# A Hymba layer on one Trainium2 core: the FFN of all four row groups by a seven-product scheme, with the products of plain weights placed beside the attention

## The chip, the core and the metric

The kernel runs on one core of a Trainium2 chip. A core has five engines that each work through their own queue in order: TensorE (PE in the profile; its weight loads are listed as PEld), VectorE (DVE), ScalarE (ACT), GpSimd (POOL) and SyncE (SP), which here issues all the transfers between DRAM and the on-chip memory. Sixteen DMA engines carry them out. The metric is device time in microseconds, lower is better. The kernel before takes 2677.42 us, the median of three runs (2672.66 to 2678.96).

## The reference

One decoder layer on 2048 rows of 1024 float32 values. Cut to what is computed:

```python
a = rmsnorm(x, g_pre_mix); u = a @ w_in                 # 1024 -> 2560
conv  = silu(layernorm(depthwise_conv31(u_val * sigmoid(u_gate)) + b))   # 512 channels
for each head and each query t:                          # 8 heads x 64
    z = q.k / 8
    A[t,s] = sigmoid(z_ts) * prod_{s<j<t} (1 - sigmoid(z_tj)),  s < t
    attn = A @ v, then a head-wise rmsnorm
h = x + rmsnorm(concat(conv, attn) @ w_out, g_post_mix)
f = rmsnorm(h, g_pre_ffn)
out = h + rmsnorm((silu(f @ w_gate) * (f @ w_up)) @ w_down, g_post_ffn)   # 1024 -> 2816 -> 1024
```

A head's attention needs a running product along each row of scores. VectorE does it with a scan, which stands between the two sigmoids on ScalarE and the multiplication on GpSimd.

## The kernel before, in words

**Precision.** Every float32 matrix product is done as three products of rounded halves (high and low part of both operands, without low by low). So a weight tile of 128 x 1024 is loaded, rounded on ScalarE and its rest taken on GpSimd (`load_w`, lines 193 to 210). The two halves are kept in DRAM and loaded from there at the next use. `Weights` (lines 212 to 225) loads two tiles ahead, into rings of three buffers.

**Row groups.** The 2048 rows are four groups of 512 rows. For each group: `prep` (operand columns), `inproj` as `gv` (gate and value of the convolution) and `qkv`, `taps` and `convnorm` (the convolution: 31 multiply-adds per channel block on VectorE, lines 437 to 485), `attn`, `mix`, `outproj`, `residual`, and the FFN.

**Attention** (lines 505 to 642). Group g has 8 heads with g+1 key blocks each; one block of 512 keys and 128 queries is called a block here, and there are 320 of them (32, 64, 96 and 128 for the four groups). A block takes: two score products (lines 533 and 536) into one of two banks `z`; two sigmoids on ScalarE (541, 543); a scan on VectorE (545); a multiplication on GpSimd (546); four transposes on TensorE (562); the rounding of the result on ScalarE and its rest on VectorE (229, 230); two products with the values (567, 568).

**The FFN of groups 0 and 1** is `ffn` (lines 701 to 844), as written: 72 products of 512 columns per 128 hidden channels (24 gate, 24 up, 24 down), 22 such steps, so 1584 for each group.

**The FFN of groups 2 and 3** is `ffn_pair` (lines 882 to 1195). The two groups are the two halves of one matrix product, which is split 2 x 2 and done by Strassen's scheme in Winograd's form: seven products instead of eight, on sums of the weights' quarters and of the inputs' quarters. The products are numbered 1 to 7 as in the code. Products 1 and 2 take plain quarters of weights and inputs; 4 takes the plain quarter 22 of the weights; 3, 5, 6 and 7 take sums of weights (lines 937 to 940). A step of gate or up is 84 products, and there are 22; the down product follows in 77 slots of 12 products (lines 1144 to 1195). Together 2772.

**The order of the work.** The table `PLAN` lists the pieces of the main chain (in-projections, out-projections, FFN). `beside` (lines 113 to 126) runs a piece step by step and lets two side chains go on: the attention of all groups and the taps. Two numbers in each row of PLAN say how far each side goes in that piece; the attention's scale (line 1204) makes its whole length 351 of these units, and the rows share them out from `prep` 0 to the last `ffn` 1. When attention and taps are over, `mix` 3 and `outproj` 3 run beside the rest of `ffn` 1 (lines 1266 to 1280), then come the pair's input sums and the pair. A scheduler orders each engine's queue afterwards from this program order; that order is fixed in the built program.

Of the kernel before, what the change touches and what calls it, by code (L numbers as in the profile page):

```python
# [19 lines left out]
P = 128  # L20
# [20 lines left out]
    ("prep", 0, 4.4, 81, ("scaled", 0, 0, 0)),  # L41
    ("gv", 0, 0, 9),
    ("qkv", 0, 0, 13, ("stats", 1, 2, 2), ("turned", 1, 15, 2)),
    ("qkv", 0, 0, 0),
    ("prep", 1, 2.4, 8),
    ("gv", 1, 10.1, 18, ("stats", 2, 0, 3)),
    ("qkv", 1, 9.9, 34),
    ("qkv", 1, 1.1, 41, ("turned", 2, 10, 6)),
    ("mix", 0, 0, 15),
    ("prep", 2, 0, 0),  # L50
    ("out", 0, 28.7, 39),
    ("qkv", 2, 7.3, 16),
    ("qkv", 2, 3.1, 19, ("residual", 0, 1, 3)),
    ("gv", 2, 25.6, 61, ("stats", 3, 0, 2)),
    ("mix", 1, 0, 1),
    ("out", 1, 0, 47, ("turned", 3, 4, 8)),
    ("prep", 3, 0, 20),
    ("qkv", 3, 5.4, 10, ("hscaled", 0, 7, 0)),
    ("qkv", 3, 0, 45),
    ("gv", 3, 14, 12, ("residual", 1, 1, 2)),  # L60
    ("fprep", 0, 12.8, 19),
    ("ffn", 0, 32.8, 16),
    ("ffn", 0, 38.2, 24),
    ("ffn", 0, 11.8, 10),
    ("ffn", 0, 20.7, 0),
    ("mix", 2, 0.6, 0),
    ("out", 2, 17.6, 0, ("hscaled", 1, 1, 0)),
    ("fprep", 1, 19.2, 0, ("residual", 2, 18, 5)),
    ("ffn", 1, 27.5, 55),
    ("ffn", 1, 26.8, 63),  # L70
    ("ffn", 1, 28.9, 45),
    ("ffn", 1, 103.6, 66),
)
LATE = 1.14
# [55 lines left out]
def layer_kernel(ctx: ExitStack, tc: tile.TileContext, x, xT, g_pre_mix, w_in, conv_w, conv_b, ln_g, ln_b,  # L130
# [129 lines left out]
    fup = C.enter_context(tc.tile_pool(name="hidden", bufs=2))  # L260
# [63 lines left out]
    def turned(T):  # L324

        g, kp = divmod(T, TT)
        if kp == 0:
            assert need(*[("stats", g * TT + t) for t in range(TT)])()
            ps = bank("tps")
            for t in range(TT):  # L330
                q = g * TT + t
                nc.tensor.transpose(ps[:, t * P:(t + 1) * P], rstd1[:, q:q + 1].to_broadcast([P, P]), id32)
            rb = fup.tile([P, G], F32, tag="uH", name="rb")
            nc.scalar.activation(rb, ps, AF.Copy)
            rbs[g] = rb
# [167 lines left out]
    pinned = [False]  # L503

    def attn(g):
# [20 lines left out]
        def scores(u, j):  # L526
# [6 lines left out]
            mz = nc.tensor.matmul(z[:, 0:w], hd_["QL"][:, js], K[:, 0:w], start=True, stop=False)  # L533
            if pinned[0]:
                tc.keep_in_program_order(mz)
# [165 lines left out]
    def ffn(g0, NT, fx, acc, up, banks, og_=lambda: ev("og"), junk_=lambda: ev("junk", BF16), more=None, rows_=None):  # L701

        two = more is not None
        pairs = not two
        HT = NT * TT
        aH = [lambda k, t=t: fx[t][0][k // 4][:, k % 4, :] for t in range(NT)]
        aL = [lambda k, t=t: fx[t][1][k // 4][:, k % 4, :] for t in range(NT)]  # L710
        srcs = []
        for f in range(NF):
            if pairs:
                srcs += [(w_gate, f), (w_up, f)] + ([(w_down, f - 1), (w_down, f)] if f % 2 else [])
            else:
                srcs += [(w_gate, f)] + ([(w_down, f - 1)] if 0 < f < NF - 1 else []) + [(w_up, f)]
        wts = Weights(srcs + ([] if pairs else [(w_down, NF - 2)]))

        def down(parts, f, tts):

            end = f + len(parts) == NF

            def block(ps, i, tt, e):
                uH, uL, WH, WL_ = parts[i]
                us = slice(tt * P, (tt + 1) * P)
                es = slice(e * G, (e + 1) * G)
                nc.tensor.matmul(ps, uL[:, us], WH[:, es], start=i == 0, stop=False)  # L727
                nc.tensor.matmul(ps, uH[:, us], WH[:, es], start=False, stop=False)  # L728
                nc.tensor.matmul(ps, uH[:, us], WL_[:, es], start=False, stop=i == len(parts) - 1)  # L729

            first = {}
            if len(parts) > 1:
                for tt, e in [(tt, e) for tt in tts for e in range(2)][:2]:
                    first[tt, e] = bank("dps")
                    block(first[tt, e], 0, tt, e)
            for tt in tts:
                ss = sp.tile([P, 2], F32, tag="ss2", name="ss2", bufs=4) if end else None
                og = []
                for e in range(2):
                    es = slice(e * G, (e + 1) * G)  # L740
                    begun = (tt, e) in first
                    ps = first[tt, e] if begun else bank("dps")
                    for i in range(begun, len(parts)):
                        block(ps, i, tt, e)
                    if f == 0:
                        nc.vector.tensor_copy(acc[tt][:, es], ps)
                    else:
                        nc.vector.tensor_tensor(acc[tt][:, es], ps, acc[tt][:, es], ALU.add)
                    if end:
                        og.append(tail(tt, e, ss))  # L750
                if end:
                    finish(tt, ss, og)
# [589 lines left out]
```

## Time and profile before

| | before |
|---|---|
| median of three runs | 2677.42 us (2672.66 to 2678.96) |
| profiled execution, its own time | 2676.57 us |
| span of that execution, first to last instruction | 2674.6 us |
| TensorE busy | 2508.3 us (94%) |
| VectorE, ScalarE, GpSimd busy | 1813.2, 1069.4, 1314.5 us (68%, 40%, 49%) |
| DMA | 556.79 MB, 208 GB/s |
| mean granted TensorE clock | 0.974 |

A row of instructions in the profile names line, engine, operation, output<-input and shape, then count, busy time and mean duration in ns, then the idle time before them and what ended it. A row of the windows names a stretch of the span, then for each engine the busy time and, in brackets, the count of instructions in it; after these stand the granted TensorE clock (1 is full speed), the busy share of the DMA engines and the rate in GB/s. Matmuls are pipelined, so the busy time of TensorE is not its work: how many it starts says more.

### The profile page before, as it was taken

To read this page: it belongs to the slowest core of one execution; us is meant where nothing else is said; L and a number is where in the kernel's file an instruction comes from. 1 tells how busy PE (TensorE), PEld (TensorE's weight loads), DVE (VectorE), ACT (ScalarE), POOL (GpSimd) and SP (SyncE) were. 2 spreads that over 40 slices of the span, in tenths; PEclk is the share of its full clock that TensorE was granted. 3 is DMA by queue.
4 is the path that set the end of the run, shared out by engine and by line. 5 is a ranking of instruction groups with operands and counts; after the bars stand their busy time and mean duration, and the time that the engine had idled before them with its cause. 6 is when DMAs were issued, how large, how long until landed. Compare 5 with 4: busy or idle time off the path is not lost.

```text
span 2674.6 us, 34465 instructions
## 1 busy us (share of the span) xinstructions
PE 2508.3 (94%) x11552; PEld 2031.6 (76%) x11552; DVE 1813.2 (68%) x2400; ACT 1069.4 (40%) x1979; POOL 1314.5 (49%) x1641
## 2 busy tenths in 40 slices
PE   8999999999999999999999999999657999999998
PEld 6788787778777787777778778887535888887886
DVE  6966698779866767554878898553257656665556
ACT  3444544454345555334564333331232222223543
POOL 4624533453155566545563322320267777674556
PEclk9999998999999999999999999999878999999999
DMA  8996776746776666666764444534433444447564
GB/s 323 347 321 229 237 265 203 258 147 225 245 281 220 229 245 232 233 244 249 252 234 170 162 169 153 186 135 177 162 117 107 135 168 161 158 142 263 189 185 170
DMA packets 200512, 556.79 MB, mean 208 GB/s; under 512 B 24720, under 2 KB 24720, under 8 KB 200336
## 3 DMA queue, kind: packets, MB, share of 16 engines
q1 hardware_dynamic: 200336, 554.61, 60.3%
q8 instruction: 91, 1.49, 0.2%
q14 instruction: 85, 0.70, 0.1%
HBM read 382.28 MB, written 172.23 MB: 207 GB/s over the span
## 4 chain that ended last, share of the span: by engine, by line
PE 63%; DVE 7%; POOL 4%; DMA 3%; ACT 2%; issue 2%; SPq 0%; POOLq 0%; DVEq 0%; ACTq 0%
PE p L950 15%; PE dps L950 7%; PE pg L237 3%; PE pg L241 3%; PE pg L239 3%; PE pu L237 3%; PE pu L239 3%; PE pu L241 3%; PE dps L727 2%; PE at L562 2%; PE dps L729 2%; PE dps L728 2%; DVE om L545 2%; PE inps L237 2%; PE inps L239 2%
## 5 line engine op out<-in xcount | busy, mean ns | idle before, releaser
L546 POOL TENSOR_TENSOR A<-A,om 128x512 f32<-128x512 f32 (+2 forms) x320 | 313.5, 980 | 663.0 <-DVE om L545 616.4
L545 DVE TENSOR_TENSOR_SCAN om<-om,one,z 128x513 f32<-128x513 f32 (+2 forms) x320 | 352.6, 1113 | 99.7 <-ACT A L543 97.7
L452 DVE SCALAR_TENSOR_TENSOR cv<-glu,cw,cv 128x512 f32<-128x512 f32 x464 | 347.2, 748 | 7.9
L206 POOL TENSOR_TENSOR wL<-raw,wH 128x1024 fp32r<-128x1024 f32 x94 | 224.6, 2394 | 143.2 <-ACT wH L205 138.3
L541 ACT ACTIVATE om<-z 128x512 f32<-128x512 f32 (+2 forms) x320 | 171.2, 536 | 249.1 <-PE z L536 149.4
L237 PE MATMUL inps<-xH,wL 128*128 128x512 f32 x640 | 258.9, 405 | 4.5 <-DVE vt L230 3.7
L239 PE MATMUL inps<-xH,wH 128*128 128x512 f32 x640 | 254.7, 399 | 0.0
L241 PE MATMUL inps<-xL,wH 128*128 128x512 f32 x640 | 254.2, 398 | 0.0
L230 DVE TENSOR_TENSOR TL<-at,TH 128x512 fp32r<-128x512 f32 (+1 forms) x320 | 187.7, 597 | 49.7 <-ACT TH L229 48.8
L229 ACT ACTIVATE TH<-at 128x512 fp32r<-128x512 f32 (+1 forms) x320 | 167.8, 545 | 122.3 <-PE at L562 117.6
L562 PE MATMUL at<-idr,A 128*128 128x128 f32 x1088 | 191.9, 276 | 4.8 <-DVE ot L584 2.4
L727 PE MATMUL dps<-wH,uL 128*128 128x512 f32 x352 | 150.0, 426 | 29.4 <-DVE uL L803 23.1
L543 ACT ACTIVATE A<-z 128x512 f32<-128x512 f32 (+2 forms) x320 | 169.7, 539 | 18.4 <-PE at L562 18.4
L562 PEld LDWEIGHTS at<-idr,A 128*128 128x128 f32 x1088 | 139.3, 142 | 41.2 <-POOL A L546 5.2
L1117 DVE TENSOR_TENSOR xLb<-lateL0b,xHb 128x512 fp32r<-128x512 f32 x77 | 99.1, 1294 | 90.9 <-ACT xHb L1116 90.9
L1115 POOL TENSOR_TENSOR t1b<-lateH0b,t0b 128x512 fp32r<-128x512 f32 x77 | 103.4, 1346 | 103.9 <-ACT t0b L1114 99.8
L205 ACT ACTIVATE wH<-raw 128x1024 fp32r<-128x1024 f32 x94 | 98.7, 1059 | 124.5 <-PE pu L241 32.6
L237 PEld LDWEIGHTS inps<-xH,wL 128*128 128x128 f32 x640 | 123.6, 193 | 30.1 <-issue 4.5
L237 PE MATMUL pu<-xH,wL 128*128 128x512 f32 x352 | 141.2, 401 | 3.9 <-DMA wL<-wL 3.2
L237 PE MATMUL pg<-xH,wL 128*128 128x512 f32 x352 | 140.9, 400 | 4.1 <-DMA wL<-wL 3.7
L241 PEld LDWEIGHTS inps<-xL,wH 128*128 128x128 f32 x640 | 123.1, 192 | 26.2
L239 PEld LDWEIGHTS inps<-xH,wH 128*128 128x128 f32 x640 | 123.5, 193 | 24.3
(308 smaller groups left out, 6559.3 us busy)
## 6 DMA issues: line engine op xcount, KB each, us to landing
wH<-wH SPq DMA_DIRECT2D x244, 512.0 KB, 4.5
wL<-wL SPq DMA_DIRECT2D x244, 512.0 KB, 4.1
raw<-in_w_gate_dram SPq DMA_DIRECT2D x44, 512.0 KB, 4.7
raw<-in_w_up_dram SPq DMA_DIRECT2D x44, 512.0 KB, 4.1
raw<-in_w_down_dram SPq DMA_DIRECT2D x44, 512.0 KB, 5.0
K<-kd SPq DMA_DIRECT2D x80, 256.0 KB, 4.1
V<-vd SPq DMA_DIRECT2D x80, 256.0 KB, 3.9
lateL0b<-ud SPq DMA_DIRECT2D x77, 256.0 KB, 2.7
```

The source lines that it names most:

```text
L206: nc.gpsimd.tensor_tensor(L, raw, H.bitcast(F32), ALU.subtract)
L230: nc.vector.tensor_tensor(L, ps, H.bitcast(F32), ALU.subtract)
L237: nc.tensor.matmul(ps, WL[:, kc], aH[t](k), start=k == 0, stop=False)
L239: nc.tensor.matmul(ps, WH[:, kc], aH[t](k), start=False, stop=False)
L241: nc.tensor.matmul(ps, WH[:, kc], aL[t](k), start=False, stop=k == KT - 1)
L452: nc.vector.scalar_tensor_tensor(to, gl[c][:, k:k + G], cw[:, c, k:k + 1], a, ALU.mult, ALU.add))
L541: nc.scalar.activation(om[:, G - w:G], z[:, 0:w], AF.Sigmoid, scale=-0.125)
L545: nc.vector.tensor_tensor_scan(r, r, z[:, 0:1].to_broadcast([P, w + 1]), one, ALU.mult, ALU.bypass)
L546: nc.gpsimd.tensor_tensor(a[:, 0:w], a[:, 0:w], om[:, G - w + 1:G + 1], ALU.mult)
L562: nc.tensor.transpose(pt[:, j * P:(j + 1) * P], u["A"][j][:, b * P:(b + 1) * P], id32)
L727: nc.tensor.matmul(ps, uL[:, us], WH[:, es], start=i == 0, stop=False)
L950: tc.keep_in_program_order(nc.tensor.matmul(ps, a, b, skip_group_check=True, **flags))
```

## The change

All four groups' FFN is done in two pairs (groups 0 and 1; groups 2 and 3) by the seven-product scheme. `ffn` and `ffn_pair` go. What is new:

- `c11(g)`: products 1 and 2 of gate and up for one pair, 528 products of 512 columns (11 steps of 48). Their results, product 1 alone and the sum of both, are copied by ScalarE into tiles of a ring of four (`ev`) and stored to DRAM, four tiles of 256 KB a step. `Weights(..., 1)` loads one tile ahead.
- `sums()`: the sums of weights, made once by GpSimd (132 operations on 128 x 512), stored, and loaded again by both pairs. It is a third side chain.
- `input_sums(g, k)`: the input sums of one pair, in four steps. Each step reads four stored pieces and stores twelve tiles, all sixteen through the ring `ev`.
- `five(g, B, todo)`: products 6, 5, 7, 3 and 4 of a step of gate or up, 60 products of 512 columns, 22 steps for a pair, with the stored sums rounded again and the results of `c11` loaded. The residuals of group 3 and the second pair's input sums run inside the first pair's steps.
- The down product of both pairs in one loop of 154 slots of 12 products.
- `PLAN` has one cost per piece instead of shares. A side chain's goal is now read off a line over the sum of these costs: ATTN runs straight from 0 at cost 80 to 1 at cost 832. The scales of the sides are given as reciprocals of their lengths; the attention's is the third line from the end of the diff below. With the yields of `attn` (unchanged), 32 x 128 for a whole unit of 512 keys and 20 x 128 for a diagonal one, the length is 2 x NH x P x sum(16 g + 10).

```diff
-    ("qkv", 3, 5.4, 10, ("hscaled", 0, 7, 0)),
-    ("qkv", 3, 0, 45),
+    ("qkv", 3, 66, ("residual", 1, 1, 3)),
+    ("fprep", 0, 6),
+    ("c11", 0, 120, ("residual", 2, 1, 1), ("hscaled", 1, 5, 0), ("tprep", 0, 6, 2), ("hscaled", 2, 19, 0)),
+    ("fprep", 2, 6),
+    ("c11", 2, 120),
...
+ATTN = ((80, 0.0), (832, 1.0))
+TAPS = ((50, 0.0), (205, 0.168), (230, 0.25), (385, 0.418), (394, 0.5), (545, 0.668), (558, 0.75), (832, 1.0))
+SUMS = ((130, 0.0), (820, 1.0))
...
+    def c11(g):
+        Hs, Ls = fx[g]
+        wts = Weights([(w, j) for j in range(HF) for w in W], 1)
+        for j in range(HF):
+            ws = [wts.next(), wts.next()]
+            pss = [bank("c11") for _ in W]
+            for hf in range(2):
+                for i, ps in enumerate(pss):
+                    WH, WL = ws[i]
+                    for k in range(4):
+                        kc = slice((4 * hf + k) * P, (4 * hf + k + 1) * P)
+                        matmul(ps, WL[:, kc], Hs[hf][:, k, :], start=hf == 0 and k == 0, stop=False)
+                        matmul(ps, WH[:, kc], Hs[hf][:, k, :], start=False, stop=False)
+                        matmul(ps, WH[:, kc], Ls[hf][:, k, :], start=False, stop=k == 3)
+                    c = ev("c")
+                    nc.scalar.activation(c, ps, AF.Copy)
+                    store(c, "c11", g, i, j, hf)
+                    yield 0.5
...
+    def input_sums(g, k, tmp):
...
+        def piece(k, i):
+            t = ev("piece")
+            nc.sync.dma_start(t, stored["fx", g, k, i])
+            return t
+        def halves(n, t):
+            H, L = ev("bH", F32R), ev("bL", F32R)
+            nc.scalar.activation(H, t, AF.Copy)
+            nc.vector.tensor_tensor(L, t, f32(H), sub)
+            store(f32(H), "B", g, n, k, 0)
+            store(f32(L), "B", g, n, k, 1)
...
+    attn_s = Side(chain(attn(g) for g in range(NG)), 1 / (8 * NH * P * sum(16 * g + 10 for g in range(NG))))
+    taps_s = Side(chain(taps(g) for g in range(NG)), 1 / (NG * (CB * CW + LAG * 3 * (1 + TT))))
+    sums_s = Side(sums(), 1 / (12 * HF))
```

What this does to the queues shows at two places. TensorE, in the attention of group 3. In the program before, score products `z`, value products `o` and transposes `at` stand among the FFN's down products `dps`:

```order
L568 MATMUL o<-TL,V 128x512
L533 MATMUL z<-K,QL 128x512
L536 MATMUL z<-K,QH 128x512
L533 MATMUL z<-K,QL 128x512
L536 MATMUL z<-K,QH 128x512
L562 MATMUL at<-idr,A 128x128 x5
L727 MATMUL dps<-wH,uL 128x512
L728 MATMUL dps<-wH,uH 128x512
L729 MATMUL dps<-wL,uH 128x512
L727 MATMUL dps<-wH,uL 128x512
L728 MATMUL dps<-wH,uH 128x512
L729 MATMUL dps<-wL,uH 128x512
```

The same engine at the same score product in the changed program:

```order
L534 MATMUL z<-K,QL 128x512
L535 MATMUL z<-K,QH 128x512
L566 MATMUL o<-TH,V 128x512
L534 MATMUL z<-K,QL 128x512
L535 MATMUL z<-K,QH 128x512
L567 MATMUL o<-TL,V 128x512
L561 MATMUL at<-idr,A 128x128 x4
L534 MATMUL z<-K,QL 128x512
L535 MATMUL z<-K,QH 128x512
L561 MATMUL at<-idr,A 128x128 x2
L534 MATMUL z<-K,QL 128x512
```

Nothing but attention stands here: its 320 blocks come ahead of out-projection 2 and of all of `c11`, and 202 of them stand in six runs with no other product between them (in the program before, 6 blocks stand so).

SyncE, beside the first pair's `c11` and `input_sums` in the changed program (`c` are the stored products, `B` the input sums, `fx` the pieces, `wH` and `wL` the kept halves of weights):

```order
L732 DMA c_0_1_2_1_14666<-c 128x512
L211 DMA wL_14747<-wL 128x1024
L211 DMA wH_14756<-wH 128x1024
L206 DMA raw<-in_w_up_dram 128x1024
L732 DMA B_3_0_0_14697<-bH 128x512
L211 DMA wL_14757<-wL 128x1024
L732 DMA B_3_0_1_14699<-bL 128x512
L206 DMA raw<-in_w_gate_dram 128x1024
L732 DMA B_5_0_0_14705<-bH 128x512
L732 DMA B_5_0_1_14707<-bL 128x512
```

and where the program before loads and stores the plain FFN's weights of group 0, among the attention's loads (`K`, `V`, `Q`):

```order
L209 DMA wH_9294<-wH 128x1024
L515 DMA QH<-qd_2_190 64x512 x2
L516 DMA QL<-qd_2_190 64x512
L209 DMA wL_9295<-wL 128x1024
L204 DMA raw<-in_w_gate_dram 128x1024
L523 DMA V<-vd_2_198 128x512
L522 DMA K<-kd_0_149 128x512
L209 DMA wH_9304<-wH 128x1024
```

The loads of weights stand now behind stores that wait for ScalarE and VectorE, and no attention work stands between them on any queue.

776 lines of the change are left out of this document (312 added, 464 removed).

## The prediction

> **What bounds the kernel now.** First the page's top line and its first part, then the windows cut where the attention's last scan ends (1771 us) and where TensorE comes to full speed again. Columns of a window: length, then busy time and count for PE, PEld, DVE, ACT, POOL, then clock, DMA share, GB/s.
>
> ```profile
> span 2674.6 us, 34465 instructions
> PE 2508.3 (94%) x11552; PEld 2031.6 (76%) x11552; DVE 1813.2 (68%) x2400; ACT 1069.4 (40%) x1979; POOL 1314.5 (49%) x1641
> 0.00:1771.00 1771.00, 1694.73 (x8090) 1379.75 (x8091) 1305.02 (x1861) 785.92 (x1525) 807.74 (x1298) 0.98 0.67 231
> 1771.00:1885.00 114.00, 106.75 (x472) 84.16 (x470) 43.15 (x65) 20.28 (x35) 5.17 (x7) 1.00 0.44 157
> 1885.00:2030.00 145.00, 81.70 (x298) 60.34 (x299) 76.34 (x78) 47.72 (x82) 82.44 (x71) 0.73 0.35 125
> 2030.00:2438.00 408.00, 401.10 (x1747) 327.75 (x1746) 256.61 (x274) 116.53 (x152) 291.77 (x165) 1.00 0.46 157
> 2438.00:2675.00 237.00, 224.06 (x948) 179.54 (x948) 132.07 (x124) 98.92 (x186) 127.33 (x101) 0.98 0.61 200
> ```
>
> TensorE looks busy everywhere but in 1885 to 2030. Its busy time overlaps itself, so I price its work by the distance of starts, from the timeline of PE in the pair and in the attention.
>
> ```profile
> 2149.70 0.62 PE L950 MATMUL p<-t4H,more 128*128 128x512 f32 x2
> 2150.15 0.39 PE L950 MATMUL p<-t4L,more 128*128 128x512 f32 x1
> 2150.38 0.62 PE L950 MATMUL p<-t4H,more 128*128 128x512 f32 x2
> ...
> 572.01 0.60 PE L562 MATMUL at<-idr,A 128*128 128x128 f32 x4
> L562 PE MATMUL at<-idr,A x1088: 269/272/476, 97.5 to 1786.7; 128*128 128x128 f32 x182
> ```
>
> Three products of 512 columns in 2150.38 - 2149.70 = 0.68 us: 0.227 us each. Four transposes take 0.60, of which the last one's length is 0.27: 0.11 each. The program before has 9524 products of 512 columns, 1644 transposes and 384 narrower products of about 0.12: 2162 + 181 + 45 = 2388 us. The span of 2675 is that work and 287 us lost. Up to the last score product stand 6144 wide ones, 1548 transposes and the 384: 1395 + 170 + 45 = 1610 us in 1771, a share of 0.91. So TensorE sets the pace while the attention runs, with FFN products between the attention's; the hole of 1885 to 2030 holds 298 products, 68 us of work in 145.
>
> **The change part by part.**
>
> *Removed.* 9128 wide products are left: 396 fewer, 90 us. The new total is 2072 + 181 + 45 = 2298 us. All the rest is what TensorE loses.
>
> *Moved: the attention.* This decides. Its scale makes its length 2/8 = 0.25 on a line that runs to 1, so it is asked for four times as fast as the line says and goes on whenever its keys are there. In the changed order only in-projections and out-projections 0 and 1 stand ahead of the last score product: 3112 wide products, 1423 transposes, the 384, or 706 + 157 + 45 = 908 us of PE work. Of it 269 us lie in the six runs of 202 blocks with nothing else. There TensorE has 1.33 us of work a block, and VectorE sets the pace:
>
> ```profile
> L545 DVE TENSOR_TENSOR_SCAN om<-om,one,z 128x513 f32<-128x513 f32 x224 | 283.0, 1272 | 85.2 <-ACT A L543 84.2 <-POOL om L540 0.4
> L230 DVE TENSOR_TENSOR TL<-at,TH 128x512 fp32r<-128x512 f32 x224 | 150.0, 678 | 44.4 <-ACT TH L229 43.6
> L452 DVE SCALAR_TENSOR_TENSOR cv<-glu,cw,cv 128x512 f32<-128x512 f32 x464 | 347.2, 748 | 7.9
> L538 DVE TENSOR_TENSOR z<-z,msk 128x128 f32<-128x128 f32 x128 | 36.1, 291 | 23.1 <-PE z L536 22.8
> 560.00:580.00 20.00, 17.47 (x90) 12.47 (x89) 17.95 (x29) 14.32 (x32) 13.30 (x30) 1.00 0.46 132
> 560.00:580.00 20.00, 8.44 (x8) 1.00 0.46 132
> 567.00:601.00 34.00, 8.45 (x8) 1.00 0.41 124
> ```
>
> In the 202 blocks VectorE has 202 scans and as many rests, 93 taps, 62 masks and some forty smaller steps in the changed order: 156 whole scans by 1.272, 152 whole rests by 0.678, 93 by 0.748, 62 by 0.291 and 81 us for the others and the shorter forms, 470 us or 2.3 us a block. The last two rows count scans alone. The densest stretch that the trace has is 8 blocks in 20 us, 2.5 us each, with VectorE 90% busy; the other had 8 in 34 us, 4.2 each. I take 2.6, near the first, since these runs have nothing else on VectorE's way: 525 us (470 to 850). The other 908 - 269 = 639 us of PE work go at the share seen, 0.91: 702 us.
>
> The sums of weights cost 69 MB of transfers, and the order starts them among the first loads. There DMA is nearly full:
>
> ```profile
> 0.00:100.00 100.00, 86.04 (x369) 69.75 (x370) 72.61 (x101) 37.74 (x53) 45.38 (x52) 0.98 0.92 329
> 100.00:200.00 100.00, 93.88 (x451) 78.00 (x450) 74.96 (x128) 43.44 (x97) 46.74 (x82) 0.97 0.96 334
> q1 hardware_dynamic: 200336, 554.61, 60.3%
> raw<-in_w_gate_dram SPq DMA_DIRECT2D x44, 512.0 KB, 4.7
> ud<-t SPq DMA_DIRECT2D x44, 256.0 KB, 4.5
> xr<-in_x_dram SPq DMA_DIRECT2D x32, 256.0 KB, 5.0
> ```
>
> About 10 MB of them fall into the first 66, 30 us at 334 GB/s; I take 20 (0 to 30). The attention so ends at 702 + 525 + 20 = 1247 us, 524 earlier than before, but with only 908 us of PE work behind it.
>
> *What is left.* 2298 - 908 = 1390 us of PE work. To it come:
>
> - `c11` 0. From its first to its last stored product SyncE moves 68 MB (stored halves 19, input sums 10, weights, `c` 11.5 and the rest), while TensorE has 123 us of work. 554.61 MB at 60.3% of 2675 us are 344 GB/s with the queues full: 68 MB need 198 us, a loss of 75. Four of its steps also hold `input_sums`: 16 tiles and 4 `c` go through a ring of four, each held for one landing (4.5 for a store, 5.0 for a load in the rows above) and some 1.5 us of work, 20 x 6 / 4 = 30 us where TensorE has 11.7: with the other seven at 13, 4 x 30 + 7 x 14 = 218. I take 100 lost (75 to 140). ScalarE's copy into the ring is the waiter; behind it on its queue stand the copies that free TensorE's banks.
> - `c11` 2: 37 MB, 108 us at that rate, beside 123: nothing, if the loads keep pace.
> - `mix` 3, out-projection 3 and the operands of products 3 and 4, whose buffers come free only with its end (16 transfers, 4.2 MB, 12 us, and a landing, less 36 products, 8 us): 25 (10 to 40).
> - The second pair's input sums through the same ring, 4 x 30 us against two steps' slack: 20 (0 to 40). The change of operands between the pairs: 10.
> - `five` and the down loop: 2640 + 1848 products, 1019 us. In 2030 to 2438 the pair does 1747 in 408, 397 us of work: 2.7% lost. 25.
> - The end, as now: 948 by 0.227 = 215 us in 237, of which the last 13 have no product: 13.
>
> The hole of 1885 to 2030 closes: the rest of `c11` 2 covers `mix` 3, and the residuals of group 3 run inside `five`. What it now loses, 77 us, is in these sums as 25 + 20.
>
> Sum: 1247 + 1390 + 100 + 25 + 20 + 10 + 25 + 13 = 2830 us of span. The profiled execution before took 2676.57 for a span of 2674.6, so 2832; it stands 0.85 under the median of the runs. I predict 2832.
>
> **The rivals.**
>
> *VectorE runs through (faster).* If banks and buffers let VectorE work ahead in the mixed parts, the attention ends by its work alone. Up to the last scan the changed order gives it 320 scans, 320 rests, 348 taps, 128 masks and 253 smaller steps, 1018 us by the durations; the same count for before gives 1375 where the window shows 1305, so 966. It has been this busy:
>
> ```profile
> 300.00:400.00 100.00, 96.54 (x469) 78.64 (x468) 93.94 (x140) 50.71 (x97) 50.72 (x72) 1.00 0.77 260
> 600.00:700.00 100.00, 96.85 (x465) 79.12 (x464) 93.94 (x139) 37.63 (x77) 34.20 (x64) 1.00 0.67 226
> ```
>
> At 0.94 the attention ends at 1028, and the kernel at 1028 + 1390 + 193 + 2 = 2613. It decides from an end of the attention before 1090 us. Against it: those windows had taps without a break, and the dense runs have 93 for 202 blocks; over 0 to 1771 VectorE stood at 0.74. Chance 0.12.
>
> *The clock gate in the dense runs.* At half clock 269 us become 538, at 0.91 592: 67 more than 525, so 2899. For it: 1885 to 2030 has a clock of 0.73. Against it: the dense 560 to 580 has 1.00 with PE half at work. Chance 0.13. The Trainium skill's "TensorE: Matmul & The Clock Gate" (Part 1 and Part 4) says that micro-idling between groups of matmuls makes the gate swing and that transposes do not count as activity; by it the time would be this rival's. The row of 560 to 580, where a third of the work is transposes, speaks against it.
>
> *Weights late in both `c11`.* `Weights` looks one tile ahead, and on SyncE's queue the loads stand behind stores that wait for copies. If every tile of `c11` 2 pays a landing,
>
> ```profile
> wH<-wH SPq DMA_DIRECT2D x244, 512.0 KB, 4.5
> ```
>
> 22 by 4.5 are 99 us more: 2931. Chance 0.14.
>
> *The change does not do what its words say:* this one is no rival but the ground of the forecast, as the order shows that attention and `c11` do not meet.
>
> **How the numbers follow.** The forecast has 0.58; the rivals 0.12, 0.13, 0.14; 0.03 is left for an end between the first rival and the forecast, near no change. A measurement of this kernel can tell 0.3% from no change, 8 us. Faster by more 0.12, within 0.03, slower 0.85. Low end: dense blocks at 2.3 (465), the mixed part at 0.94 (680), `c11` 0 at 75 and the small ones at 65: 465 + 680 + 10 + 1390 + 75 + 65 = 2685. High end: dense at 3.2 (646), the start at 30, `c11` at 140, the small ones at 75, 702 + 646 + 30 + 1390 + 140 + 75 = 2983. Range 2690 to 2980; the two later rivals lie in it, the first is left out.
>
> **What would show it.** Right: the last scan at about 1250 us; some 400 fewer matmul records than before's 11552; windows before it with VectorE at 0.8 or more and TensorE at half its usual count, above all in the last 92 blocks; then a stretch of some 220 us with a DMA share over 0.9 and 528 products; from the start of `five` some 1050 us with TensorE as now. Wrong: a last scan before 1090 (VectorE ran through) or after 1400; clock records under 0.8 in the dense runs (the gate); a DMA share under 0.8 in `c11` 0 with TensorE at full count (the ring and the queue cost nothing); a share under 0.9 of TensorE in `five`.

## The result and the profile after

The changed kernel takes 3191.65 us, the median of four runs (3189.44 to 3192.52), where the kernel before takes 2677.67 us (four runs). The ratio is 1.1922, with a 95% interval of 1.1902 to 1.1943. The forecast had the sign, but its 2832 us are 360 short and its range ended at 2980. The profiled execution took 3192.33 us for a span of 3190.6.

The top of the page of the changed kernel, then its windows, cut at the places that the forecast priced: the runs of pure attention of groups 1 to 3 (316 to 483, 748 to 954, 1196 to 1466), the first product behind the attention (1466), the first pair's `c11` (1556 to 1811), `five` (1997 to 2745) and the down product. The columns are those of the windows before.

```profile
span 3190.6 us, 36148 instructions
PE 2630.6 (82%) x11156; PEld 2017.4 (63%) x11156; DVE 1856.9 (58%) x2447; ACT 1191.6 (37%) x2179; POOL 1363.9 (43%) x1718
```

```profile
0.00:316.00 316.00, 282.62 (x1292) 227.09 (x1292) 169.71 (x281) 131.93 (x269) 174.25 (x259) 0.95 0.98 338
316.00:483.00 167.00, 106.27 (x415) 68.83 (x413) 128.13 (x191) 76.25 (x161) 118.22 (x197) 0.78 0.59 192
483.00:748.00 265.00, 221.87 (x955) 173.64 (x954) 150.59 (x205) 94.76 (x182) 151.37 (x198) 0.91 0.85 298
748.00:954.00 206.00, 133.49 (x563) 85.72 (x562) 163.47 (x225) 104.78 (x217) 101.32 (x217) 0.86 0.26 79
954.00:1196.00 242.00, 217.43 (x974) 171.75 (x974) 152.54 (x216) 90.08 (x179) 77.83 (x148) 0.94 0.61 202
1196.00:1466.00 270.00, 187.56 (x775) 118.42 (x774) 217.21 (x285) 149.75 (x303) 126.75 (x288) 0.88 0.18 55
1466.00:1556.00 90.00, 76.40 (x326) 58.63 (x326) 53.56 (x80) 25.03 (x40) 16.77 (x15) 0.90 0.44 155
1556.00:1811.00 255.00, 153.88 (x593) 119.46 (x594) 109.13 (x141) 72.60 (x112) 73.73 (x51) 0.79 0.81 297
1811.00:1997.00 186.00, 176.87 (x751) 139.99 (x751) 23.68 (x36) 45.52 (x77) 14.68 (x17) 0.98 0.79 282
1997.00:2745.00 748.00, 649.34 (x2675) 505.55 (x2674) 428.83 (x563) 199.53 (x265) 243.23 (x120) 0.97 0.60 203
2745.00:3191.00 446.00, 424.90 (x1850) 348.37 (x1848) 260.04 (x231) 201.41 (x380) 265.76 (x210) 0.98 0.65 212
```

TensorE's count fell by 396, as the order said (11552 to 11156), and its loss grew by far more than that. Set beside the terms of the forecast:

| stretch | forecast, us | measured, us | more |
|---|---|---|---|
| to the first product behind the attention | 702 + 525 + 20 = 1247 | 1466 | 219 |
| from there to `five` | 371 of work + 100 + 25 = 496 | 531 | 35 |
| `five` | 599 of work + 16 + 20 + 10 = 645 | 748 | 103 |
| down product and end | 420 of work + 9 + 13 = 442 | 446 | 4 |

So three fifths of the error of 361 us lie beside the attention, and most of the rest in `five`. Three of the forecast's own signs of being wrong came up: the last scan ends at 1430, behind its 1400; one of the dense runs below holds 9 us at a clock of 0.50; and in `five` TensorE's share is 0.81 by the forecast's prices (603 us of work in 748).

The attention's last scans in groups 1, 2 and 3 end at 450, 918 and 1430 us. First the scans alone in the three dense runs up to there (length, VectorE's busy time with the count, clock, DMA share and GB/s), then the tails behind them with all columns:

```profile
316.00:450.00 134.00, 50.29 (x48) 0.81 0.61 200
748.00:918.00 170.00, 74.56 (x66) 0.92 0.31 95
1196.00:1430.00 234.00, 108.92 (x94) 0.93 0.21 64
450.00:483.00 33.00, 9.21 (x43) 6.07 (x41) 17.05 (x24) 4.58 (x9) 17.58 (x21) 0.66 0.50 159
918.00:954.00 36.00, 9.49 (x32) 6.11 (x32) 25.18 (x35) 4.19 (x7) 3.87 (x9) 0.58 0.00 1
1430.00:1466.00 36.00, 9.19 (x31) 5.93 (x31) 25.67 (x37) 6.27 (x11) 3.66 (x7) 0.58 0.00 0
```

Up to the last scans there are 208 in 538 us, 2.6 us each: the forecast's price for a dense block holds. What it had not priced are the tails, 105 us in which the attention's scans are over and TensorE starts next to nothing (106 products and transposes, 0.12 to 0.17 of the time by the forecast's prices). It waits there not for scans but for `lps`, `po` and `cps`, as its waits up to 1500 us show (releaser, us in total, times, longest):

```profile
PE z L534 <- DVE om L544: 101.9, 180, 1.6
PE lps L468 <- DVE acc L454: 48.6, 4, 19.8
PE po L599 <- DVE ot L591: 40.7, 12, 12.8
PE cps L485 <- POOL cs L480: 29.2, 7, 9.1
PE o L567 <- DVE TL L232: 22.5, 65, 1.7
```

`lps` and `cps` belong to the convolution's layer norm, which comes behind the last tap `acc` of a channel block; `po` belongs to the attention's own norm. The timeline of all engines at the end of group 1's attention (rows between these are left out):

```profile
461.21 0.69 DVE L589 TENSOR_REDUCE ss<-sq 128x8 f32<-128x512 f32 x1 [0.76 <-ACT sq L587]
...
466.17 1.26 POOL L773 TENSOR_TENSOR sum<-sum 128x512 f32<-128x512 f32 x1 [3.51 <-DMA sum<-in_w_gate_dram]
467.51 0.20 POOL L184 TENSOR_SCALAR msa<-ss 128x8 f32<-128x8 f32 x1
...
470.69 1.74 DVE L591 TENSOR_TENSOR ot<-ot,ss 128x512 f32<-128x512 f32 x1 [8.79 <-POOL ss L185]
472.35 9.45 DVE L454 SCALAR_TENSOR_TENSOR cv<-glu,cw,cv 128x512 f32<-128x512 f32 x12
...
482.64 0.48 PE L468 MATMUL lps<-idr,acc 128*128 128x128 f32 x1 [8.98 <-DVE acc L454]
```

The attention's norm is ready on VectorE at 461.9, but GpSimd takes its step at 467.5, behind sums of weights that wait for their transfers. VectorE's queue is in order, so twelve taps stand behind that, and TensorE's `lps` behind the last of them. It matters whose taps these are: they are still group 0's. With the layer norm and the mix behind them they are what out-projection 0 lacks (experiment 12 tests this), and they end at 482, when the attention of group 1 is already done. The taps up to the first out-projection (first the changed kernel, then the kernel before; same columns as the scans):

```profile
0.00:100.00 100.00, 9.82 (x13) 0.97 0.99 357
100.00:233.00 133.00, 28.39 (x38) 0.92 0.99 336
233.00:450.00 217.00, 41.70 (x56) 0.87 0.74 245
450.00:535.00 85.00, 9.81 (x13) 0.72 0.57 196
```

```profile
0.00:100.00 100.00, 51.32 (x69) 0.98 0.92 329
100.00:233.00 133.00, 38.79 (x52) 0.97 0.89 308
233.00:314.00 81.00, 0.74 (x1) 0.98 0.72 235
```

Before, group 0's taps are over at 233 us and out-projection 0 starts at 314. Changed, more than half of them are still to come at 233 (69 of the 120 in these rows), and out-projection 0 starts at 535 (TensorE's first rows of the `ops` products, before and changed):

```profile
L661 PE MATMUL ops<-wH,xL x192: 387/390/629, 313.9 to 1362.8; 128*128 128x512 f32 x192
```

```profile
L660 PE MATMUL ops<-wH,xL x192: 390/393/792, 535.0 to 1543.9; 128*128 128x512 f32 x192
```

### The profile page after: what moved, and what is told of

It reads as the page before. It is cut to its first block, busy times and chain, and to the rows that moved or that the text cites. A ratio compares the mean times of both kernels' runs of the same rounds, so it can differ in the third digit from the quotient of the medians.

```text
span 3190.6 us, 36148 instructions
## 1 busy us (share of the span) xinstructions
PE 2630.6 (82%) x11156; PEld 2017.4 (63%) x11156; DVE 1856.9 (58%) x2447; ACT 1191.6 (37%) x2179; POOL 1363.9 (43%) x1718
## 5 line engine op out<-in xcount | busy, mean ns | idle before, releaser
L963 POOL TENSOR_TENSOR wL<-raw,wH 128x1024 fp32r<-128x1024 f32 x88 | 213.2, 2423 | 516.3 <-ACT wH L962 479.3
L1078 DVE TENSOR_TENSOR xL__22139<-t__22141,xH__22138 128x512 fp32r<-128x512 f32 x154 | 198.9, 1298 | 163.6 <-ACT xH__22138 L1077 163.6
L239 PE MATMUL inps<-xH,wL 128*128 128x512 f32 x640 | 268.7, 420 | 28.7 <-ACT vs L406 14.0
L1076 POOL TENSOR_TENSOR xL__22137<-t__22140,xH__22136 128x512 fp32r<-128x512 f32 x154 | 207.6, 1352 | 181.5 <-ACT xH__22136 L1075 171.1
L726 PE MATMUL dps<-xH__22136,xL__22139 128*128 128x512 f32 x616 | 241.7, 392 | 8.8 <-DVE xL__22139 L1078 7.2
L726 PE MATMUL dps<-xL__22137,xH__22138 128*128 128x512 f32 x616 | 241.2, 392 | 2.3 <-POOL xL__22137 L1076 2.3
L726 PE MATMUL dps<-xH__22136,xH__22138 128*128 128x512 f32 x616 | 241.0, 391 | 0.0
L534 PE MATMUL z<-K,QL 128*128 128x512 f32 (+2 forms) x320 | 148.2, 464 | 106.7 <-DVE om L544 101.9
L773 POOL TENSOR_TENSOR sum<-sum 128x512 f32<-128x512 f32 x132 | 171.9, 1302 | 143.5 <-DMA sum<-in_w_down_dram 48.0
L726 PE MATMUL c<-xH,wL 128*128 128x512 f32 x352 | 149.1, 424 | 98.5 <-ACT c L761 94.1
L561 PE MATMUL at<-idr,A 128*128 128x128 f32 x1088 | 203.3, 298 | 11.3 <-POOL A L545 7.7
L208 POOL TENSOR_TENSOR wL<-raw,wH 128x1024 fp32r<-128x1024 f32 x50 | 121.4, 2430 | 211.1 <-ACT wH L207 201.0
L561 PEld LDWEIGHTS at<-idr,A 128*128 128x128 f32 x1088 | 149.9, 153 | 51.6 <-POOL A L545 14.2
```

The costliest lines, as they stand in the source:

```text
L239: nc.tensor.matmul(ps, WL[:, kc], aH[t](k), start=k == 0, stop=False)
L561: nc.tensor.transpose(pt[:, j * P:(j + 1) * P], u["A"][j][:, b * P:(b + 1) * P], id32)
L726: return nc.tensor.matmul(ps, a, b, skip_group_check=True, **flags)
L963: nc.gpsimd.tensor_tensor(L, r, f32(H), sub)
L1076: nc.gpsimd.tensor_tensor(WL, w, f32(WH), sub)
L1078: nc.vector.tensor_tensor(UL, t, f32(UH), sub)
```

## The experiments

Fifteen kernels ran. Unless it is said otherwise, each is the changed kernel with the edit shown, and its time is a single one, beside 2666 to 2675 us of the kernel before on the same chip; a difference of less than 10 us between two chips is therefore not read as one.

**1. The attention's scale.**

```diff
-    attn_s = Side(chain(attn(g) for g in range(NG)), 1 / (8 * NH * P * sum(16 * g + 10 for g in range(NG))))
+    attn_s = Side(chain(attn(g) for g in range(NG)), 1 / (2 * NH * P * sum(16 * g + 10 for g in range(NG))))
```

> The changed kernel with one figure changed: the attention's scale takes 2 in place of 8, so that its length is 1.0 on the line and not 0.25. In the order the last score product then stands behind 3747 products of 512 columns in place of 3111, with 372 of c11 among them, and 123 blocks in place of 202 stand in runs of pure attention. Theory (the rushed attention leaves TensorE waiting for VectorE in the dense runs and leaves c11 bare): last scan at about 1450 us with 1052 us of TensorE work up to it in place of 908, behind it 1246 us of work and between 270 and 370 us of losses, 2960 to 3070 us in all. Rival (the losses lie behind the attention, and VectorE needs as long for it wherever it stands): 3190 within 30. Second rival (the line is right as it is for VectorE, and spreading the attention makes the taps and the mixes late): over 3220.

Measured: 2869.75 us, 322 less. The last scan ends at 1447, as expected (1430 in the changed kernel), but `five` starts at 1677 in place of 1997, and takes as long as it did (746). Up to 1500 us the trace has none of TensorE's waits for `lps` left, and those for `cps` and `po` fall from 29.2 and 40.7 us to 7.2 and 10.9. The sign is the theory's, the size is beyond its range: the two `c11` now begin at 1163 and are over at 1623, and 411 of their 1056 products start before the last scan, where it was none. Both rivals fall.

**2. The rush alone, in the kernel before.**

```diff
-    attn_s = Side(chain(attn(g) for g in range(NG)), 1.26e-3)
+    attn_s = Side(chain(attn(g) for g in range(NG)), 1.26e-3 / 4)
```

> The kernel before with nothing changed but the attention's scale, a quarter of what it was, so that its attention is asked for four times as fast, as in the changed kernel. In the order the last score product then stands behind 3183 products of 512 columns in place of 6143, and 163 blocks in place of 6 stand in runs of pure attention. FFN, weights and transfers are as before. Theory (rushing the attention is by itself most of the loss): TensorE loses some 300 to 400 us more, 2980 to 3080 us. Rival (the attention costs VectorE the same wherever it stands, and the excess of the changed kernel comes from the new FFN pieces): 2680 to 2780 us. The forecast's own prices (dense blocks at 2.6 us, the rest at a share of 0.91) would make it 2850 to 2950.

Measured: 3037.01 us beside 2674.9: 362 lost with the old FFN, old transfers and old prices. So the rush is a loss by itself, of the size that undoing it gives back (322). The forecast's own prices fail here too. The late taps are less of it than in the changed kernel: TensorE's waits up to 1500 us for `lps`, `cps` and `po` are 14.6, 11.8 and 18.0 us here. What makes up the rest of the 362 was not taken apart.

**3. The bank order in `five`.** Product 5's bank `b3` is read before product 7, and product 7's step on VectorE is then one, not two.

```diff
-                product(b2, 7, A, B, False)
                 u3 = next(u_)
-                nc.vector.tensor_tensor(u3, b2, s1, add)
-                nc.vector.tensor_tensor(u3, b3, u3, add)
+                nc.vector.tensor_tensor(u3, b3, s1, add)
+                product(b2, 7, A, B, False)
+                nc.vector.tensor_tensor(u3, b2, u3, add)
```

> The changed kernel, where five adds the stored product to the bank of product 5 before product 7 and not after it, so that product 3 finds its bank read already. One step of VectorE then stands between product 7 and the next use of a bank in place of two. Theory (product 3 waits about 1.5 us for two VectorE steps in each of 44 steps): 66 us less, 3125 us, and five from 748 us to about 685. Rival (the wait moves to product 4 or to the next step's banks, since VectorE has the same work): less than 20 us gained, 3172 or more.

Measured: 3118.91 us, 73 less. The waits of TensorE between 2300 and 2600 us, first changed, then with the edit, and the window of all of `five` with the edit:

```profile
PE b L726 <- DVE cs L1020: 15.1, 10, 1.5
PE b L726 <- DVE accf L1020: 13.6, 9, 1.5
PE b L726 <- DVE cy L1013: 2.1, 8, 0.3
```

```profile
PE b L726 <- DVE cy L1013: 2.6, 10, 0.4
PE b L726 <- DMA e__19861<-B: 2.5, 1, 2.5
```

```profile
2004.00:2671.00 667.00, 632.45 (x2675) 502.79 (x2675) 424.95 (x559) 198.66 (x264) 243.34 (x120) 0.98 0.67 225
```

(`cs` and `accf` at line 1020 are `u3`.) Nineteen waits of 1.5 us in 300 us are gone, and `five` takes 667 in place of 748: 81 less. In all of `five` the waits at line 1020 sum to 71.8 us in 42 records, and to 3.6 with the edit, so some 13 us of the 81 are not these waits. The rival falls.

**4. The ring of the input sums.** In the first pair's `c11` the pieces use the attention's tag `A`, the halves its tags `TH` and `TL`:

```diff
-            t = ev("piece")
+            t = ap.tile([P, G], F32, tag="A", name="piece", bufs=NA) if early else ev("piece")
...
-            H, L = ev("bH", F32R), ev("bL", F32R)
+            if early:
+                H, L = (ap.tile([P, G], F32R, tag=t_, name=n_) for t_, n_ in (("TH", "bH"), ("TL", "bL")))
+            else:
+                H, L = ev("bH", F32R), ev("bL", F32R)
```

> The changed kernel, where the first pair's input sums take their tiles from rings of the attention that are out of use by then (pieces from a ring of six, the halves from two rings of two), so that the products of c11 have the ring of four to themselves. Every transfer stays. Theory (the ring of four holds ScalarE, and it the banks of TensorE): c11 of the first pair from 248 us to 150 to 170, 3090 to 3120 us in all. Rival (the 68 MB on SyncE's queue need 198 us at the highest rate seen): 200 or more for this stage, 3140 to 3190 us. Second rival (the wait is for weights behind stores): no change, 3190 within 10.

Measured: 3141.72 us, 50 less. The waits of TensorE in this stage, changed and with the edit, and the stage with the edit:

```profile
PE c L726 <- ACT c L761: 92.3, 8, 19.6
```

```profile
PE c L726 <- ACT c L761: 35.5, 12, 12.9
PE c L726 <- ACT tmp L826: 15.8, 4, 13.0
```

```profile
1556.00:1768.00 212.00, 154.22 (x591) 117.65 (x592) 114.13 (x145) 74.18 (x115) 72.19 (x51) 0.85 0.93 352
```

The stage takes 212 in place of 255 us, and with the ring out of the way DMA is 93% busy at 352 GB/s. That is the first rival's range: the ring is worth 43 us, and what is left is near the 198 us that the transfers need at 344 GB/s. That they are what holds the stage now is argued from this rate and was not tried by moving fewer bytes.

**5. The sums later.** The first three tiles are written from a result of group 0's attention before they are loaded, so no sum can start sooner.

```diff
-SUMS = ((130, 0.0), (820, 1.0))
+SUMS = ((400, 0.0), (820, 1.0))
...
+        first = [ma[0, 3]] * 3
...
+            if first:
+                nc.gpsimd.tensor_copy(t[:, 0:1], first.pop()[:, 0:1])
```

> The changed kernel, where the first three tiles of the sums of weights wait for the attention of group 0 to be over, so that none of their transfers falls into the first 400 us. All else stays, the 69 MB and the 132 GpSimd operations among it. Theory of the forecast (the sums cost some 20 us at the start, where DMA is full, and nothing else): 3165 to 3175 us, first 316 us of work done in about 295. Rival (what counts is GpSimd: its small steps for the layer norm and the attention's norm stand behind sums that wait for transfers, in the bare ends of groups 0 and 1): 3130 to 3160. Second rival (they only cost later, when they come): 3180 to 3200.

Measured: 3165.03 us, 27 less. The first 316 us, to set beside the first window above:

```profile
0.00:316.00 316.00, 286.94 (x1362) 229.58 (x1362) 192.93 (x322) 146.15 (x299) 155.97 (x270) 0.99 0.92 312
```

70 more products start in them. The forecast's 20 for the start holds in size. In the ends of the groups little changed: out-projection 0 starts 285 us behind group 0's last scan, where it was 303.

**6. Nearly no sums.** Twelve sums in place of 132, used for all tiles, so that the output is not the layer's; the edit for the down product is of the same kind.

```diff
-        for j in range(HF):
+        for j in range(1):
...
-                    nc.sync.dma_start(t, stored["S", i, j, n])
+                    nc.sync.dma_start(t, stored["S", i, 0, n])
```

> The changed kernel with sums of weights made only for the first of the 11 tiles and used for all: it leaves out 120 of the 132 sums with their loads and stores, so that its output is not the reference's. Loads in five and in the down product stay as many. Theory (the sums cost 20 us at the start): 3170. Rival (they hold GpSimd's queue and the transfers all through the first 780 us): 60 to 110 us, 3080 to 3130.

Measured: 3123.26 us, 68 less, in the rival's range. None of it is the start: the twelve sums that are left come in the first 114 us, and 1298 products start in the first 316 us, where it was 1292. So the 68 are what the other sums cost later, beside the 27 of experiment 5. The last scan ends at 1381, and 50 of the 68 are gained ahead of it. TensorE's waits up to 1500 us for `po` and `cps`, which stand behind GpSimd's small steps, fall from 40.7 and 29.2 us to 22.1 and 18.4; those for `lps` stay at 48.6.

**7. Scale and bank order together.**

> The changed kernel with both edits of the first two runs: the attention's scale with 2, and in five the bank of product 5 read before product 7. The two act at different times (the first up to about 1450 us, the second behind the attention). Theory (they add up): 2870 less 72 is 2798, between 2785 and 2805. Rival (with the attention spread, something else is late in five, such as the loads of weights and sums, at a DMA share of 0.6): 2840 or more.

Measured: 2793.85 us. The two edits add up (2798 expected), so they are two losses.

**8. Scale, bank order and ring.**

> The changed kernel with the attention's scale with 2, the bank of product 5 read before product 7, and the first pair's input sums in the attention's rings. In the order 960 of the 1056 products of c11 now stand ahead of the last score product, in place of 372. Theory (as without the spread, the ring gives back some 40 us, and more of c11 lies beside the attention): 2730 to 2765. Rival (the rings are in use by the attention now, which waits for the input sums' stores): 2800 or more.

Measured: 2776.91 us, 17 under the last one, between the theory and the rival: the ring gives back less where the attention uses the same tiles.

**9. The input sums spread**, on kernel 7.

```diff
-("tprep", 0, 6, 2)
+("tprep", 0, 6, 4)
...
-            todo[t + TT + 1] = [(input_sums, NG - 2, t, tmp)]
+            todo[3 * t + TT + 1] = [(input_sums, NG - 2, t, tmp)]
...
-        todo[2 * TT + 1] = [(second,)]
+        todo[4 * TT + 1] = [(second,)]
```

> The changed kernel with the attention's scale with 2 and the bank of product 5 read before product 7, and the input sums spread: the first pair's four steps stand at every fourth half step of c11 in place of every second, the second pair's at every third step of five in place of every one. Theory (each step takes some 30 us through the ring of four however it is placed, and a pair of steps of c11 or three of five cover it): 30 to 60 us under 2794, 2735 to 2765. Rival (the c tiles of c11 use the same ring, and lose the same time at whatever place): 2785 to 2800.

Measured: 2780.59 us, 13 less, outside both ranges. All of it is gained in `five`, which starts at 1678 us in both kernels: its first quarter takes 172 us in place of 191, the other three 5 more. The first pair's spreading in `c11` gains nothing, as the rival has it.

**10. The sums later as well**, on kernel 9.

> The last kernel, and the sums of weights begin when the attention of group 0 is over, as in the run with the late sums. Theory (the 25 us at the start come back, as they did there): 2710 to 2740, 25 under the last kernel. Rival (with the attention spread, DMA is fuller beside c11, and the sums now collide with it): within 10 of the last kernel or above it.

Measured: 2779.56 us, 1 less. That is the rival's range: what the late sums save at the start, they cost later here. That they collide with the transfers beside `c11` is the rival's reason and was not looked into.

**11. The ring as well**, on kernel 10.

> The last kernel, and the first pair's input sums in the attention's rings. Theory (c11 keeps its ring, and more of it stands beside the attention): 2690 to 2720. Rival (the attention now waits for the input sums' stores): over 2730.

Measured: 2755.17 us, 24 less, in the rival's range.

**12. The taps early, with the rush as it is.** Only the table of the taps changes:

```diff
-TAPS = ((50, 0.0), (205, 0.168), (230, 0.25), (385, 0.418), (394, 0.5), (545, 0.668), (558, 0.75), (832, 1.0))
+TAPS = ((15, 0.0), (100, 0.168), (150, 0.25), (232, 0.25), (320, 0.418), (365, 0.5), (396, 0.5), (485, 0.668),
+        (530, 0.75), (560, 0.75), (700, 0.918), (780, 1.0))
```

> The changed kernel with only the line of the taps changed: each group's taps and layer norm are asked for soon after the group's values are there (group 0 by cost 150 of its mix at 232, and so on), in place of evenly up to the mix. The attention is as rushed as before. In the order 112 blocks in place of 202 stand in runs of pure attention. Theory now (a mix waits for taps that VectorE has behind the rushed attention of the next group, and the out-projection and the next in-projection wait for the mix): out-projection 0 from 535 us to 330 to 400, and 80 to 150 us less in all, 3040 to 3110. Rival (the rushed attention by itself fills VectorE, and early taps only move the wait): 3160 to 3200.

Measured: 2939.36 us, 252 less, more than expected. Its taps in the first 411 us, and the start of its out-projections:

```profile
0.00:100.00 100.00, 53.59 (x71) 0.96 0.96 341
100.00:222.00 122.00, 36.33 (x49) 0.85 0.90 316
222.00:411.00 189.00, 0.00 (x0) 0.95 0.88 296
```

```profile
L660 PE MATMUL ops<-wH,xL x192: 390/395/775, 410.5 to 1264.2; 128*128 128x512 f32 x192
```

Group 0's taps are over by 222 us and out-projection 0 starts at 411 in place of 535, and out-projections 1 and 2 at 800 and 1204 in place of 986 and 1498. TensorE's waits up to 1500 us for `lps`, `cps` and `po` fall from 48.6, 29.2 and 40.7 us to 0.6, 0.8 and 10.2. `five` starts at 1744 in place of 1997 and takes 746: all of the gain lies ahead of it. The last scan ends at 1356. The built order changes with the table, as the expectation says: 112 blocks stand alone in place of 202, so the run tests the table of the taps and not the waits alone.

**13. Scale and early taps, nothing else.**

> The changed kernel with only the attention's scale with 2 and the early line of the taps. Each alone gave 320 and 252 us. Theory (both cure the same wait, of mixes and out-projections for taps behind the attention on VectorE): they overlap, 2830 to 2870. Rival (two separate losses, the dense blocks and the late taps): 2620 to 2700.

Measured: 2893.11 us, above both ranges. Alone the edits give 322 and 252, together 299, so they do not add up: they cure in the main the same loss, and both take the same waits away. With the scale already at 2 the early taps cost 23 us; the last scan then ends at 1519 in place of 1447. Why is open.

**14. Kernel 11 with the early taps.**

> The kernel with the attention's scale with 2, the bank order in five, the input sums spread and in the attention's rings and the late sums (2755 us), and the line of the taps as in the other run. Theory (the ends of groups 0 to 2 close here as well): 2660 to 2700, level with the kernel before. Rival (with the attention spread the taps were not what the mixes waited for): 2745 to 2765.

Measured: 2750.32 us, 5 less, the rival's range, which fits experiment 13.

**15. The first pair's `c11` ahead of mix 2**, on kernel 14, with the residuals of group 2 behind out-projection 2 and the taps of groups 2 and 3 asked for by cost 620 and 832.

```diff
-    ("gv", 3, 44),
-    ("mix", 2, 0),
-    ("out", 2, 48, ("hscaled", 0, 4, 0)),
+    ("gv", 3, 44, ("hscaled", 0, 4, 0)),
     ("fprep", 0, 6),
-    ("c11", 0, 120, ("residual", 2, 1, 1), ("hscaled", 1, 5, 0), ("tprep", 0, 6, 4), ("hscaled", 2, 19, 0)),
-    ("fprep", 2, 6),
+    ("c11", 0, 120, ("hscaled", 1, 5, 0), ("tprep", 0, 6, 4)),
+    ("mix", 2, 0),
+    ("out", 2, 48),
+    ("fprep", 2, 6, ("residual", 2, 0, 0), ("hscaled", 2, 0, 0)),
```

> The 2750 us kernel with c11 of the first pair moved ahead of mix 2 and out-projection 2, so that its 528 products stand beside the attention of group 3 and the taps of group 2. Theory (what is left against the kernel before is that TensorE has too little other work while VectorE does attention and taps: it loses 380 us before five there, against 238 up to the hole's end before): 30 to 80 us less, 2670 to 2720. Rival (VectorE's own work sets the end of the attention, wherever c11 stands): 2735 to 2765. Second rival (c11 with its input sums now makes out-projection 2 late): over 2765.

Measured: 2729.47 us, the median of four (2719.72 to 2732.3), 21 less than kernel 14 and between the theory and the rival. The ratio to the kernel before is 1.0192 (1.0167 to 1.0216). No version beats the kernel before. Its window up to `five`:

```profile
0.00:1640.00 1640.00, 1468.92 (x6681) 1148.71 (x6682) 1163.97 (x1659) 782.38 (x1540) 882.65 (x1398) 0.94 0.79 270
```

VectorE is busy 71% and DMA 79%: neither is full, and neither of the two theories explains the 57 us that remain. By the forecast's prices, as an estimate, this kernel has 90 us less of TensorE's work than the one before and loses some 350 us ahead of `five`, where the kernel before loses some 250 up to the end of its hole at 2030; the rest of the difference lies behind these places. What holds this repaired kernel above the one before stays open.

## Why the prediction was wrong, point by point

**The ground was right.** Attention and `c11` do not meet, because the attention's length is a quarter of its line; undoing that gives 322 us (experiment 1), and doing it to the kernel before costs 362 (experiment 2).

**The step that failed** is in the part on the attention: "The other 908 - 269 = 639 us of PE work go at the share seen, 0.91: 702 us", beside "I take 2.6 ... 525 us" and 20 for the start. The mixed part with the start measured 823 us in place of 722, the dense runs with their tails 643 in place of 525. The 2.6 us held in the dense runs themselves, 538 us for 208 blocks. What failed is the share (639 us of work in 823 are 0.78), and the tacit step under both, that the taps keep up: the sum has no term for the ends of the groups, which took 105 us.

The line `TAPS` stands in the diff as well, and I did not price it. It asks for a group's taps evenly up to the cost of its mix, while the attention is asked for four times too early. VectorE works through its queue in order, so more than half of group 0's taps come only after 233 us, between the scans of group 1's attention. Mix 0 waits for them, out-projection 0 for the mix, and the next in-projection stands behind it on TensorE. Experiment 12 shows that this table is what costs: with only the table changed and the attention asked for as early as before, 252 us come back, and the waits for the layer norm go. Experiment 13 shows that this gain and that of the attention's scale are in the main the same one. How the 101 us of the mixed part divide between late taps, transfers and other waits was not separated.

A smaller part is GpSimd's: its small norm steps stand behind sums that wait for transfers. The forecast's 20 for the start of the sums held in size (27 in experiment 5), but without most of the sums another 50 us come back ahead of the last scan (experiment 6), for which the forecast had nothing; TensorE's waits for `po` and `cps` shrink by 29 us there. The rest of the 50 was not separated.

**The second step that failed** is "2.7% lost. 25", which I took from the program before for `five` and the down product. The down product had it (446 against 442). In `five`, product 3 adds to a bank that VectorE must have read, by two steps that can start only behind product 7: 1.5 us, 44 times. The code stood in the change, and the old pair's share could not show it. Experiment 3 gives 81 us of the 103 for one moved line. With it the four quarters of `five` take 190, 159, 161 and 156 us; the first is where the second pair's input sums run, and spreading these brought it to 172 in experiment 9.

**`c11` 0** was right in its parts and 32 short: 255 in place of 223. The ring is there with 43 us (experiment 4), and the rate of 352 GB/s without it speaks for SyncE's transfers as most of the rest. In the ring's sum the forecast says 13 us for a step and adds up 14, which is 7 us too much. `c11` 2 costs hardly anything beyond its work, as forecast: it runs from 1811 to 1941, 130 us for the forecast's 123 of work.

**The rivals.** VectorE did not run through: in 0 to 1466 its windows above sum to 982 us, 67%. The weights are not late in both `c11`: 1811 to 1997 has 751 products and transposes in 186 us at a clock of 0.98. The clock gate's rival had something in it and not its price. The dense runs have 0.81, 0.92 and 0.93; inside the first the clock once stood at half for 9 us, though TensorE's waits in 330 to 346 are 2.7 us at most:

```profile
337.00:346.00 9.00, 5.37 (x17) 3.59 (x17) 5.15 (x10) 2.60 (x6) 6.41 (x11) 0.50 0.65 206
```

A block took 2.8, 2.6 and 2.5 us in the three, so if the lower clock is what slowed the first, it cost some 12 us there (48 blocks by 0.25, an estimate from these rows), where the rival had 67. The Trainium skill's "TensorE: Matmul & The Clock Gate" (Part 4) says that a transpose does not count as busy in the way that a product does. More than a third of TensorE's work is transposes in all three runs (by the forecast's prices), and two of them keep 0.92 and 0.93, so the transposes alone did not hold the clock down here. The lowest clocks, 0.58 to 0.66, stand in the tails, where TensorE waits up to 20 us for VectorE; how much the low clock adds to them was not tried.

**The range** left out the case that came true, since all my rivals that were slower kept the share of 0.91 in the mixed parts. With 0.78, as it was with the start's loss in it, the same sum has 819 us for them, and 819 + 525 = 1344 at the end of the attention; only with the high end's 646 for the dense blocks, which it had for slower blocks and not for tails, does it come to 1465.

## What to carry to other kernels

When a change moves the goals of several side chains, price every line, not only the one that moves most: two chains that share an engine in order delay each other, and here the one that a later product waits for, the taps, decided. A share of busy time must not be carried from a program whose gaps were filled by other work to one where that work stands elsewhere. Where one bank takes several products in turn and is read between them, do the reading that depends on the older product first, so that only one short step stands between two products.

## What the hardware showed that I had not expected

- Where VectorE reads a bank in the middle of its sum, TensorE's next product on that bank waited 1.5 us for its two steps: taking one of the two out of the wait, 44 times, gave 81 us in `five`. The Trainium skill's "PSUM — Partial Sum Buffer" (section "The four PSUM rules") says that the hardware allows such a synchronised read; the rows at line 1020 put its price beside it.
- The DMA engines carried 352 GB/s over 212 us at a share of 0.93 in experiment 4, and 338 over the first 316 us of the changed kernel, near the 344 that the forecast took for full queues.
- With more than a third of TensorE's work in transposes the mean clock stayed at 0.92 and 0.93 over 170 and 234 us of attention alone. Single stretches of it fell to half without a long wait (0.50 in 337 to 346, no wait over 2.7 us there), and the tails with waits up to 20 us had 0.58 to 0.66.
